# A decoder block's branch projections moved from the attention into the gate pairs, with the first stage reordered and the pooling spread

## The chip, the cores and the metric

The kernel runs on one core of one Trainium2 chip. The metric is the device time of one execution in microseconds (us). Engines are named as in the profile: PE (TensorE, matmuls) with PEld (its weight loads), DVE (VectorE), ACT (ScalarE), POOL (GpSimd), SP (SyncE, which issues most DMAs).

## The reference

One layer on x of 1024 positions by 1024 channels, float32:

```python
h = rmsnorm(x, attn_norm_g)
z = h @ w_in                       # u, v | xb | q | k | values
gates = sigmoid(h @ w_gate + b_gate)
y_a = gmlp_mixer(z[..., :512])     # gelu, layer norm, causal 128x128 mixing
y_b = pool_mixer(z[..., 512:768])  # causal means over 2, 4, 8, 16 positions, 64x64 maps
y_c = diff_attn_mixer(...)         # 4 heads, difference of two softmaxes
merged = g_a * (y_a @ proj_a) + g_b * (y_b @ proj_b) + g_c * (y_c @ proj_c)
x = x + merged @ w_out
x = x + conv_ffn(rmsnorm(x, ffn_norm_g), ...)
return rmsnorm(x, final_norm_g)
```

`proj_a` and `proj_b` are 256 x 1024, `w_gate` is 1024 x 3072 (1024 columns for each of the branches a, b and c).

## The kernel before

Activations lie transposed: a tile has 128 channels by 1024 positions. Each fp32 operand is split into a high and a low part (`split`: an ACT cast and a DVE subtraction), and a product is three matmuls of 512 columns (`mm3`, L189, which records at L191: high x high, high x low, low x high).

`strassen_pair` (L253) multiplies two 128-column blocks of a weight with h by a Winograd form: seven products of twelve matmuls, A11·B11, S1·T1, S2·T2, A12·B21, S3·T3, A22·T4 and S4·B22, which come to stand in the banks b1 to b4. ACT copies b1 after some of them (`c`), DVE adds the copy and another bank (`add`, L262) into the results F1 and F2. S4·B22 goes on top of bank b3, so it waits until b3 has been read into F2, which needs the copy taken after S3·T3. Between products the function calls `mid()`, through which other work can be put in. `prepare` (L226) loads a pair's weights (r1, r2), forms the sums s1, s2 on POOL (L234 to L237) and splits everything; these tiles come from a pool of 13 (`w4`), results from a pool of 34 (`a4`).

The stages, in order of time:
- First stage, up to 118 us: projections for u and v of branch a in two halves of positions, with `scaled` (L314, cast `hb` and its rest), `squares` (L326, ACT) and `factors` (L337: the sums of squares and 1/rms R8, by ACT's square root for the first half and by DVE alone for the second), `bcast_rows` (RB, the factor of each position), `u_gelu`, `v_gelu`, the relative bias `rel_bias` (L380), then the attention's values by Winograd products (T tiles from `h.winograd`).
- The pair with branch b's input `zb`, then three pairs for q and k. `pooling` (L602) is a generator of DVE steps over `zb`: at each `mid` of the first of these pairs two steps are taken. `store_qk` (L671) multiplies by RB (`times_r`, L349), splits and stores to DRAM. `pool_outs` does branch b's small products and stores y_d[2..3]; `gating` has stored branch a's y_d[0..1].
- Twelve gate pairs, about 205 to 435: `strassen_pair`, `times_r` on POOL (L351), a sigmoid on ACT (L771), a store to g_d. g_d 0 to 7 are the gates of branch a, 8 to 15 of b, 16 to 23 of c.
- The last pair of q and k, and the attention, 447 to 602: 35 steps over 32 tiles. In each step `next(filler)` (L1222) does one unit of `merge_ab` (L1164): six matmuls of a branch's projection (`mm`), and DVE's product with the loaded gate tile (L1174). After both branches of a tile an accumulating DMA adds gb to ga.
- Branch c's merge, `w_out`, and the feed-forward part, which the change does not touch.

The order of each engine's instructions is set by the tile framework, which schedules the program with a timeline of its own; `tc.issue_after(x)` holds a group behind the instruction x, `tc.high_priority()` puts one ahead.

## Time and profile before

| | |
|---|---|
| time, median of 3 runs | 1393.08 us (1388.32 to 1394.64) |
| profiled execution | 1393.11 us, its span 1391.4 us |
| granted clock of PE, mean | 0.989 |
| busy: PE, DVE, ACT, POOL | 1346.7, 966.5, 653.0, 496.3 us |
| DMA | 204.63 MB, mean 147 GB/s |

The profile is one execution. Busy times are shares of the span. A timeline row gives start, duration, engine, line, operation, tiles and shapes, and in brackets how long the engine sat idle before it and what released it; rows of a line's group give the count, the busy time, the mean of one in ns, and the idle time ahead. PEclk is the granted clock, 1.00 for 2.4 GHz.

### The profile page before, as it was taken

What the parts mean: (1) busy time and instruction counts of PE and PEld (TensorE: products, weight loads), DVE (VectorE), ACT (ScalarE), POOL (GpSimd) and SP (SyncE); (2) the same over time, 40 slices, a digit from 0 to 9 for tenths busy, and PEclk for the clock granted to TensorE, in tenths of its full rate; (3) what the DMA queues carried; (4) which work ended last, traced back from release to release, by engine and by line L of the source; (5) the groups of instructions that cost most, each with busy time, mean ns of one, the idle gap of its engine ahead of it and who ended that gap; (6) DMA issues with size and microseconds to landing.
All of it is one profiled execution on the core that took longest, in us unless ns stands there. A gap on an engine that the chain in (4) does not pass through costs nothing.

```text
span 1391.4 us, 17681 instructions
## 1 busy us (share of the span) xinstructions
PE 1346.7 (97%) x6454; PEld 1124.1 (81%) x6454; DVE 966.5 (69%) x1481; ACT 653.0 (47%) x1110; POOL 496.3 (36%) x327
## 2 busy tenths in 40 slices
PE   8999899999999889999999999999999999999997
PEld 7888678888888678878878888888888887878786
DVE  7585755544444789967869667667767669985863
ACT  8443244433344567742676443333334336455461
POOL 0005334555553100012231566666666640102014
PEclk9999999999999999999999999999999999999998
DMA  7222244333337898498795222222222248945853
GB/s 262 68 58 108 101 147 151 116 106 111 116 122 184 271 266 232 130 272 189 204 235 122 91 76 88 70 85 91 76 92 79 75 144 303 292 123 150 225 128 124
DMA packets 78830, 204.63 MB, mean 147 GB/s; under 512 B 8270, under 2 KB 17614, under 8 KB 78744
## 3 DMA queue, kind: packets, MB, share of 16 engines
q1 hardware_dynamic: 67224, 180.44, 39.2%
q0 software_dynamic: 11520, 23.07, 9.5%
q8 instruction: 50, 0.82, 0.2%
q14 instruction: 36, 0.29, 0.1%
HBM read 143.70 MB, written 47.46 MB: 137 GB/s over the span
## 4 chain that ended last, share of the span: by engine, by line
PE 68%; DVE 14%; DMA 8%; issue 6%; ACT 3%; POOL 1%; SPq 0%; DVEq 0%; POOLq 0%; ACTq 0%
PE b L191 63%; DMA x<-in_xT 2%; PE mm L191 1%; DMA fr<-in_w_down 1%; DVE sc L757 1%; DVE ft L97 1%; DVE fw L97 1%; DMA qs<-qk_d 1%; DMA fr<-in_w_out 1%; DMA pr<-in_w_proj 1%; PE ms L1107 1%; POOL ga L104 1%; DMA yr<-y_d 1%; ACT fw L96 1%; DMA act<-act_d 1%
## 5 line engine op out<-in xcount | busy, mean ns | idle before, releaser
L191 PE MATMUL b<-ft,fw 128*128 128x512 f32 (+1 forms) x1308 | 293.4, 384 | 6.1 <-ACT ft L96 1.9
L191 PEld LDWEIGHTS b<-ft,fw 128*128 128x128 f32 x1308 | 240.0, 189 | 56.9 <-DVE fw L97 3.2
L351 POOL TENSOR_TENSOR F<-F,RB 128x1024 f32<-128x1024 f32 x68 | 188.5, 2774 | 142.5 <-DVE F L262 141.1
L191 PE MATMUL b<-hb,Ah 128*128 128x512 f32 x608 | 188.8, 390 | 0.0
L262 DVE TENSOR_TENSOR F<-b,c 128x512 f32<-128x512 f32 x152 | 100.8, 682 | 122.4 <-ACT c L281 68.9
L191 PE MATMUL b<-T,Sh 128*128 128x512 f32 x504 | 155.7, 389 | 0.4 <-ACT c L272 0.4
L191 PEld LDWEIGHTS b<-hb,Ah 128*128 128x128 f32 x608 | 114.3, 188 | 23.7
L97 DVE TENSOR_TENSOR Al<-r,Ah 128x1024 fp32r<-128x1024 f32 x38 | 52.2, 1373 | 101.1 <-issue 77.4
L234 POOL TENSOR_TENSOR s<-r 128x512 f32<-128x512 f32 x36 | 54.4, 1512 | 189.1 <-DMA r<-in_w_up 88.9
L191 PE MATMUL b<-hb,Al 128*128 128x512 f32 x304 | 118.3, 389 | 0.0
L97 DVE TENSOR_TENSOR Sl<-s,Sh 128x1024 fp32r<-128x1024 f32 x76 | 109.2, 1437 | 11.7 <-PE b L191 6.1
L96 ACT CAST Sh<-s 128x1024 fp32r<-128x1024 f32 x76 | 80.1, 1053 | 79.4 <-PE b L191 47.5
L191 PEld LDWEIGHTS b<-T,Sh 128*128 128x128 f32 x504 | 94.5, 188 | 20.5 <-ACT c L272 0.8
L191 PE MATMUL b<-hb,Sh 128*128 128x512 f32 x304 | 95.8, 397 | 8.1 <-DVE F L262 8.1
L191 PE MATMUL b<-T,Sl 128*128 128x512 f32 x252 | 98.1, 389 | 0.0
L96 ACT CAST Ah<-r 128x1024 fp32r<-128x1024 f32 x38 | 39.9, 1050 | 109.3 <-PE b L191 104.2
L96 ACT CAST fw<-fr 128x512 fp32r<-128x512 f32 x90 | 54.7, 622 | 60.1 <-DVE fw L97 23.9
L191 PE MATMUL b<-Tl,Sh 128*128 128x512 f32 x204 | 79.4, 389 | 0.0
L191 PE MATMUL b<-Th,Sh 128*128 128x512 f32 x204 | 78.8, 391 | 0.0
L191 PE MATMUL b<-Th,Sl 128*128 128x512 f32 x204 | 78.2, 389 | 0.0
L191 PEld LDWEIGHTS b<-hb,Sh 128*128 128x128 f32 x304 | 57.9, 191 | 21.3 <-DVE F L262 9.4
L97 DVE TENSOR_TENSOR A<-r,A 128x512 fp32r<-128x512 f32 x38 | 72.3, 1904 | 0.0
(284 smaller groups left out, 2829.6 us busy)
## 6 DMA issues: line engine op xcount, KB each, us to landing
fr<-in_w_down SPq DMA_DIRECT2D x47, 512.0 KB, 4.6
r<-in_w_up SPq DMA_DIRECT2D x42, 512.0 KB, 3.6
r<-in_w_gate SPq DMA_DIRECT2D x24, 512.0 KB, 3.8
g_d<-F SPq DMA_DIRECT2D x24, 512.0 KB, 2.6
act_d<-cv SPq DMA_DIRECT2D x22, 512.0 KB, 2.6
act<-act_d SPq DMA_DIRECT2D x22, 512.0 KB, 7.4
fr<-in_w_out SPq DMA_DIRECT2D x18, 512.0 KB, 4.6
ssb<-sq POOLq DMA_DIRECT2D x24, 256.0 KB, 4.1
```

The source lines that it names most:

```text
L96: nc.scalar.copy(hi, src)
L97: (eng or nc.vector).tensor_tensor(out=lo, in0=src, in1=hi.bitcast(F32), op=ALU.subtract)
L104: nc.gpsimd.dma_start(out=dst, in_=src, accum_op=ALU.add)
L191: last_mm[0] = nc.tensor.matmul(ps, lhsT=w[a], rhs=x[b], start=first and i == 0, stop=last and i == 2, skip_group_check=more)
L234: eng.tensor_tensor(out=s1[:, :NH], in0=a21, in1=a22, op=ALU.add)
L262: nc.vector.tensor_tensor(out=o, in0=ps, in1=c, op=ALU.add)
L351: (eng or nc.gpsimd).tensor_tensor(out=F, in0=F, in1=RB, op=ALU.mult)
L757: nc.vector.tensor_tensor_reduce(out=sc_[:, c0:c0 + n], in0=ps[:, :n], in1=H["T"][:, o:o + n], scale=1.0, scalar=mx[:, 0:1] if n_ else 3.0e38,
L1107: nc.tensor.matmul(po[:, :P], lhsT=AH[t][:, kb, :], rhs=H["V"][:, kb, :], start=kb == 0, stop=kb == i)
```

## The change

- First stage: the squares follow the last high cast of their half (`last_hi`); 1/rms of the first half no longer uses ACT's square root; `rel_bias` moves behind the pair of `zb`; the differences in `h.winograd` follow the first half's factors (`r8_done`).
- Pooling: one step at each `mid`, over the first two q/k pairs; `pool_outs` follows in the third.
- Gate pairs 0 to 3 (branch a's gates): the branch's two values (`load_y`) and, for each pair, a weight block (`load_branch`) are loaded; behind a pair, `branch` multiplies 4 x 6 matmuls, two banks of PSUM (`m`) taking turns, and DVE multiplies the gates by them. It is handed on as the `mid` of the next pair, and what is left is done at that pair's end. `times_r` of these pairs is on DVE, F2 ahead of F1, and g_d gets the products instead of the gates.
- Attention: the filler has branch b only, 16 units in place of 32; the accumulating DMA adds g_d[m] from DRAM to gb; two values and four weight blocks are loaded instead of four and eight.

```diff
--- before.py
+++ after.py
@@ -311,11 +311,13 @@
         if j == 1 and kt == 0:
             tc.keep_in_program_order(i)
 
+    last_hi, r8_done = [None], [None, None]
+
     def scaled(kt, j):
 
         src = xt[kt][:, half(j)]
         t = a4([P, 2, NH], F32R, "hb")
-        nc.scalar.mul(t[:, 0, :], src, col(C_GA + kt))
+        last_hi[0] = nc.scalar.mul(t[:, 0, :], src, col(C_GA + kt))
         nc.vector.scalar_tensor_tensor(out=t[:, 1, :], in0=src, scalar=col(C_GA + kt), in1=t[:, 0, :].bitcast(F32),
                                        op0=ALU.mult, op1=ALU.subtract)
         h.b[kt][j] = t[:, 0, :], t[:, 1, :]
@@ -328,7 +330,8 @@
         k = 2 * j + kt % 2
         src = xt[kt][:, half(j)]
         sq = c2("acc" if kt < 2 else "sq")
-        nc.scalar.activation(out=sq, in_=src, func=AF.Square)
+        with tc.issue_after(last_hi[0].ins):
+            nc.scalar.activation(out=sq, in_=src, func=AF.Square)
         if kt < 2:
             acc[k] = sq
         else:
@@ -341,7 +344,7 @@
             ss_cols(ps, acc[2 * j], 4, 1, 0)
             t = tiny(4, "ssum")
             nc.vector.tensor_scalar(out=t, in0=ps[:, :4], scalar1=1.0 / D, scalar2=1e-6, op0=ALU.mult, op1=ALU.add)
-            nc.vector.tensor_copy(R8[:, 4 * j:4 * j + 4], rsqrt(t, 4, j == 0))
+            r8_done[j] = nc.vector.tensor_copy(R8[:, 4 * j:4 * j + 4], rsqrt(t, 4, False))
 
     def gain(kt):
         nc.scalar.mul(xt[kt], xt[kt], col(C_GA + kt))
@@ -466,7 +469,6 @@
         else:
             w_V = load_V()
             wk, wsm, pbd = load_wide()
-            rel_bias()
             factors(1)
             pv = [v_part(1, 0)]
         with tc.high_priority():
@@ -651,8 +653,10 @@
             nc.scalar.mul(yb, pb, col(C_PS + f))
             nc.sync.dma_start(out=y_d[2 + f, :, half(j)], in_=yb)
 
-    for j in range(4):
-        h.winograd(xt, j)
+
+    with tc.issue_after(r8_done[0].ins):
+        for j in range(4):
+            h.winograd(xt, j)
     vs = values()
     next(vs)
     layer_norm()
@@ -667,6 +671,8 @@
     for z in zb:
         times_r(z, nc.vector)
 
+    rel_bias()
+
 
     def store_qk(i, Fs, eng=None):
         for n_, F in enumerate(Fs):
@@ -689,11 +695,10 @@
         ops = prepare(w_qk[1 + i])
         if i == 0:
             pl = pooling(zb)
-        store_qk(i, strassen_pair(ops, h, pb1, lambda: (next(pl, None), next(pl, None))), nc.vector)
-        if i == 0:
+        store_qk(i, strassen_pair(ops, h, pb1, lambda: next(pl, None)), nc.vector)
+        if i == 1:
             for _ in pl:
                 pass
-        if i == 1:
             pl = pool_outs()
 
     for _ in pl:
@@ -763,13 +768,55 @@
         nc.scalar.activation(out=sc_[:, :W], in_=sc_[:, :W], func=AF.Exp, bias=nm_, scale=-1.0, accum_out=sum_)
         st[t]["s"].append(sum_)
 
+    def load_y(i):
+
+        alloc = a4 if i % 2 == 0 else w4
+        hi, lo = alloc([P, 2, NH], F32R, "yv"), alloc([P, 2, NH], F32R, "yv")
+        for j in range(2):
+            raw = c2("yr")
+            nc.sync.dma_start(out=raw, in_=y_d[i, :, half(j)])
+            split(hi[:, j, :], lo[:, j, :], raw)
+        return [(hi[:, j, :], lo[:, j, :]) for j in range(2)]
+
+    def load_branch(n):
+
+        m, g = 2 * n % 8, 2 * (n // 4)
+        raw = c2("pr")
+        nc.sync.dma_start(out=raw.rearrange("p (m a b) -> p m a b", m=2, a=2),
+                          in_=w_proj[m:m + 2, :, g:g + 2, :].rearrange("m p a b -> p m a b"))
+        hl = w4([P, 2, NH], F32R, "ph")
+        split(hl[:, 0, :], hl[:, 1, :], raw)
+        return hl[:, 0, :], hl[:, 1, :]
+
+    def branch(n, Fs, whl, yb):
+
+        for k in (1, 0):
+            F = Fs[k]
+            for j in range(2):
+                ps = pm1()
+                for ki in range(2):
+                    mm3(ps, wsl(whl, 2 * k + ki), yb[ki][j], ki == 0, ki == 1)
+                nc.vector.tensor_tensor(out=F[:, half(j)], in0=ps, in1=F[:, half(j)], op=ALU.mult)
+                if j == 1:
+                    nc.sync.dma_start(out=g_d[2 * n + k], in_=F)
+                yield
+
+    br = iter(())
     for n_ in range(12):
-        Fs = strassen_pair(w_gate[n_], h, pb1)
-        for k, F in enumerate(Fs):
+        if n_ == 0:
+            yb = [load_y(i) for i in range(2)]
+        if n_ < 4:
+            whl = load_branch(n_)
+        Fs = strassen_pair(w_gate[n_], h, pb1, lambda: next(br, None))
+        for _ in br:
+            pass
+        for k, F in reversed(list(enumerate(Fs))):
             m = 2 * n_ + k
-            times_r(F)
+            times_r(F, nc.vector if n_ < 4 else None)
             nc.scalar.activation(out=F, in_=F, func=AF.Sigmoid, bias=col(C_BG + m), scale=1.0)
-            nc.sync.dma_start(out=g_d[m], in_=F)
+            if n_ >= 4:
+                nc.sync.dma_start(out=g_d[m], in_=F)
+        br = branch(n_, Fs, whl, yb) if n_ < 4 else iter(())
 
 
     zero = tiny(1, "zero", 1)
@@ -1156,26 +1203,24 @@
 
     def ab(m):
         if m not in abs_:
-            abs_[m] = a4(n="ga"), a4(n="gb"), load_p(m, 0)
-            nc.sync.dma_start(out=abs_[m][0], in_=g_d[m])
-            nc.sync.dma_start(out=abs_[m][1], in_=g_d[8 + m])
+            abs_[m] = a4(n="gb"), load_branch(4 + m // 2) if m % 2 == 0 else abs_[m - 1][1]
+            nc.sync.dma_start(out=abs_[m][0], in_=g_d[8 + m])
         return abs_[m]
 
     def merge_ab():
         for m in range(KT):
-            ga, gb, whl = ab(m)
+            gb, whl = ab(m)
             for j in range(2):
                 if j == 1 and m < KT - 1:
                     ab(m + 1)
-                for g, k in ((ga, 0), (gb, 2)):
-                    ps = pmm()
-                    for ki in range(2):
-                        mm3(ps, wsl(whl, k + ki), yab[k + ki][j], ki == 0, ki == 1)
-                    nc.vector.tensor_tensor(out=g[:, half(j)], in0=ps, in1=g[:, half(j)], op=ALU.mult)
-                    if (g, j) == (gb, 1):
-                        accumulate(ga, gb)
-                        mg.append(ga)
-                    yield
+                ps = pmm()
+                for ki in range(2):
+                    mm3(ps, wsl(whl, 2 * (m % 2) + ki), yab[ki][j], ki == 0, ki == 1)
+                nc.vector.tensor_tensor(out=gb[:, half(j)], in0=ps, in1=gb[:, half(j)], op=ALU.mult)
+                if j == 1:
+                    accumulate(gb, g_d[m])
+                    mg.append(gb)
+                yield
 
     filler = merge_ab()
     avs = iter(())
@@ -1207,7 +1252,7 @@
     for t in range(len(tiles) + 3):
         hd, i = tiles[min(t, 31)]
         if t == 0:
-            yab = [load_yab(i) for i in range(4)]
+            yab = [load_yab(2 + i) for i in range(2)]
         if t == 2:
             store_qk(NHEAD - 1, last_qk)
         if t % 8 == 3 and t < 24:
@@ -1218,7 +1263,7 @@
             scores(t, 0)
         transpose(t - 2, 0)
         next(avs, None)
-        if t >= 1:
+        if t in (1, 2, 3) or t % 2 == 0:
             next(filler, None)
         scores(t, 1)
         combine(t - 1)
```

Three places show how instructions move.

**DVE in the first q/k pair.** `pw` are the tiles of the pooling steps; F_210 (before) and F_208 (after) are the pair's F2, whose first sum S4·B22 waits for. Before:

```order
L615 TENSOR_TENSOR pw_1511<-pw_1492 128x1022
L620 TENSOR_TENSOR h_207_1487<-h_207_1487,F_183_1338 128x16
L614 COPY pw_1514<-pw_1511 128x4
L615 TENSOR_TENSOR pw_1514<-pw_1511 128x1020
L621 SCALAR_TENSOR_TENSOR F_183_1338<-pw_1468,cs,F_183_1338 128x1024
L614 COPY pw_1531<-pw_1514 64x8
L615 TENSOR_TENSOR pw_1531<-pw_1514 64x1016
L623 COPY F_183_1338<-h_207_1487 128x16
L262 TENSOR_TENSOR F_210_1509<-b_1438,c_1507 128x512
L262 TENSOR_TENSOR F_210_1509<-b_1517,c_1507 128x512
```

After:

```order
L262 TENSOR_TENSOR F_204_1473<-b_1474,c_1441 128x512
L625 COPY F_174_1318<-h_209_1508 128x16
L97 TENSOR_TENSOR Al_1568<-r_216_1557,Ah_1567 128x1024
L97 TENSOR_TENSOR Sl_1572<-s_218_1561,Sh_1571 128x1024
L97 TENSOR_TENSOR A_224_1575<-r_217_1558,A_224_1575 128x512
L97 TENSOR_TENSOR Sl_1579<-s_219_1562,Sh_1578 128x1024
L616 COPY pw_1624<-pw_1527 128x2
L617 TENSOR_TENSOR pw_1624<-pw_1527 128x1022
L262 TENSOR_TENSOR F_208_1506<-b_1443,c_1504 128x512
L262 TENSOR_TENSOR F_208_1506<-b_1513,c_1504 128x512
L616 COPY pw_1642<-pw_1624 128x4
L617 TENSOR_TENSOR pw_1642<-pw_1624 128x1020
```

Ten pooling instructions stood between the pair's first sum and F2's; now the next pair's four splits and three pooling instructions do.

**SP between the q/k pairs and the gate pairs.** `qh` and `ql` are the split results of a q/k pair, `yb` branch b's values, `yr` the reads of branch a's values, `pr` a projection's weights. Before:

```order
L229 DMA r_244_1706<-in_w_qk 128x1024
L230 DMA r_245_1707<-in_w_qk 128x1024
L679 DMA qk_d<-qh_1554 128x1024
L680 DMA qk_d<-ql_1555 128x1024
L679 DMA qk_d<-qh_1561 128x1024
L680 DMA qk_d<-ql_1562 128x1024
L229 DMA r_276_1865<-in_w_gate 128x1024
L230 DMA r_277_1866<-in_w_gate 128x1024
L229 DMA r_296_1996<-in_w_gate 128x1024
```

After:

```order
L777 DMA yr_1876<-y_d 128x512
L777 DMA yr_1882<-y_d 128x512
L777 DMA yr_1886<-y_d 128x512
L785 DMA pr_1890<-in_w_proj 128x2x256
L685 DMA qk_d<-qh_1857 128x1024
L229 DMA r_286_1895<-in_w_gate 128x1024
L230 DMA r_287_1896<-in_w_gate 128x1024
L686 DMA qk_d<-ql_1858 128x1024
L685 DMA qk_d<-qh_1864 128x1024
```

The first gate weights stood behind the stores of the first q/k pair (`qh_1554` to `ql_1562`); now behind the first store of the third one (`qh_1857`).

**PE at the end of a gate pair.** In before this is gate pair 1's end: b_2036 is its bank b3, with S4·B22 on hb and Sh; b_2225 and b_2152 belong to the pair behind it. Before:

```order
L191 MATMUL b_2225<-Th_700,A_324_2145 128x512
L191 MATMUL b_2225<-Tl_701,A_324_2145 128x512
L191 MATMUL b_2225<-Th_700,A_324_2145 128x512
L191 MATMUL b_2225<-Th_712,A_324_2145 128x512
L191 MATMUL b_2152<-Th_700,Sh_2141 128x512
L191 MATMUL b_2152<-Tl_701,Sh_2141 128x512
L191 MATMUL b_2036<-hb_346,Sh_2017 128x512 x2
L191 MATMUL b_2036<-hb_346,Sl_2018 128x512
L191 MATMUL b_2036<-hb_349,Sh_2017 128x512 x2
```

After, gate pair 1's end: b_2054<-Th,Sh is the end of S3·T3, b_2069 the bank b3, m_2312 the third unit of the branch:

```order
L191 MATMUL b_2054<-Th_711,Sh_2050 128x512
L191 MATMUL b_2054<-Tl_712,Sh_2050 128x512
L191 MATMUL b_2054<-Th_711,Sl_2051 128x512
L191 MATMUL b_2069<-hb_351,Sh_2050 128x512 x2
L191 MATMUL b_2069<-hb_351,Sl_2051 128x512
L191 MATMUL b_2069<-hb_354,Sh_2050 128x512 x2
L191 MATMUL b_2069<-hb_354,Sl_2051 128x512
L191 MATMUL b_2069<-hb_357,Sh_2050 128x512 x2
L191 MATMUL b_2069<-hb_357,Sl_2051 128x512
L191 MATMUL b_2069<-hb_360,Sh_2050 128x512 x2
L191 MATMUL b_2069<-hb_360,Sl_2051 128x512
L191 MATMUL m_2312<-yv_1870,ph_2026 128x512
```

S4·B22 stood among the products of the pair behind it; now it follows its own pair's S3·T3, and the branch's matmuls follow it.

## Rows read from the trace of the kernel before

**Rows 1.** Engine line of the page: busy us (share of the span) xinstructions.

```profile
PE 1346.7 (97%) x6454; PEld 1124.1 (81%) x6454; DVE 966.5 (69%) x1481; ACT 653.0 (47%) x1110; POOL 496.3 (36%) x327
```

**Rows 2.** By stretch: us; busy PE, PEld, DVE, ACT, POOL; PEclk, DMA share, GB/s.

```profile
175.00:210.00 35.00, 35.00 (x148) 27.56 (x148) 20.20 (x20) 13.97 (x19) 12.24 (x10) 1.00 0.43 156
455.00:490.00 35.00, 29.57 (x160) 24.34 (x159) 24.75 (x63) 19.93 (x47) 5.81 (x3) 0.95 0.85 267
490.00:525.00 35.00, 30.59 (x195) 25.82 (x194) 30.90 (x101) 22.91 (x67) 1.73 (x2) 1.00 1.03 258
525.00:560.00 35.00, 34.66 (x220) 30.00 (x219) 32.38 (x104) 24.49 (x76) 1.72 (x2) 1.00 0.88 232
560.00:595.00 35.00, 35.00 (x231) 31.42 (x230) 33.28 (x108) 25.74 (x77) 1.72 (x2) 1.00 0.45 135
447.00:602.00 155.00, 142.34 (x862) 121.54 (x861) 129.34 (x408) 101.97 (x291) 12.29 (x11) 0.99 0.81 223
```

**Rows 3.** Timeline of PE: start, us, instruction, in brackets the idle time ahead and releaser.

```profile
13.65 1.28 PE L191 MATMUL b<-hb,wh 128*128 128x512 f32 x3 [1.81 <-ACT hb L318]
49.76 0.58 PE L191 MATMUL b<-wh,hb 128*128 128x256 f32 x1 [1.88 <-ACT vg L429]
159.43 1.22 PE L191 MATMUL b<-hb,Sh 128*128 128x512 f32 x2 [5.49 <-DVE F L262]
453.96 0.73 PE L191 MATMUL b<-hb,Sh 128*128 128x512 f32 x2 [1.40 <-DVE F L262]
```

**Rows 4.** Busy time by stretch again, around and behind the stalls of PE.

```profile
70.00:105.00 35.00, 32.69 (x245) 31.48 (x245) 30.19 (x50) 16.59 (x25) 1.43 (x2) 0.95 0.21 62
13.65:19.00 5.35, 5.30 (x15) 3.90 (x16) 5.35 (x10) 5.35 (x9) 0.00 (x0) 0.68 1.01 367
49.80:52.70 2.90, 2.90 (x14) 2.90 (x14) 1.60 (x8) 2.12 (x5) 0.00 (x0) 0.50 0.03 9
159.50:165.00 5.50, 5.50 (x13) 4.39 (x14) 4.42 (x8) 1.91 (x3) 0.62 (x1) 0.50 0.00 0
454.00:456.00 2.00, 2.00 (x9) 1.66 (x10) 1.78 (x5) 0.00 (x0) 0.80 (x1) 1.00 1.05 389
```

**Rows 5.** Timeline of DVE, first qk pair: a pooling step, and the sum behind them all.

```profile
146.06 1.21 DVE L615 TENSOR_TENSOR pw<-F 128x1023 f32<-128x1023 f32 x1
158.70 1.27 DVE L262 TENSOR_TENSOR F<-b,c 128x512 f32<-128x512 f32 x2
```

**Rows 6.** Timeline of PE, thirteen matmuls of 512 columns without a gap.

```profile
1157.11 3.11 PE L191 MATMUL b<-ft,fw 128*128 128x512 f32 x13
```

**Rows 7.** SyncE's issue of the first gate weights; the page's group of such loads.

```profile
178.94 0.33 SPq L229 DMA_DIRECT2D r<-in_w_gate  x1
...
r<-in_w_gate SPq DMA_DIRECT2D x24, 512.0 KB, 3.8
```

**Rows 8.** Durations: DVE groups 144 to 215, ScalarE groups 175 to 435, one DVE instruction.

```profile
L262 DVE TENSOR_TENSOR F<-b,c 128x512 f32<-128x512 f32 x13 | 8.7, 685 | 19.7 <-PE b L191 10.9 <-ACT c L281 8.7
...
187.17 1.23 DVE L351 TENSOR_TENSOR F<-F,RB 128x1024 f32<-128x1024 f32 x1
...
L96 ACT CAST Ah<-r 128x1024 fp32r<-128x1024 f32 x13 | 13.6, 1045 | 26.7 <-PE b L191 26.7
L771 ACT ACTIVATE F<-F,cs 128x1024 f32<-128x1024 f32 x22 | 25.4, 1155 | 37.9 <-POOL F L351 37.9
```

**Rows 9.** Timeline of GpSimd: two sums of weight blocks.

```profile
154.24 2.24 POOL L236 TENSOR_TENSOR s<-r,r 128x512 f32<-128x512 f32 x1
183.84 1.29 POOL L234 TENSOR_TENSOR s<-r 128x512 f32<-128x512 f32 x1 [6.05 <-DMA r<-in_w_gate]
```

**Rows 10.** DVE groups in the attention, 447 to 602.

```profile
L1174 DVE TENSOR_TENSOR ga<-mm,ga 128x512 f32<-128x512 f32 x16 | 11.0, 686 | 4.8 <-DMA ga<-g_d 2.7 <-PE mm L191 1.9
L97 DVE TENSOR_TENSOR ph<-pr,ph 128x512 fp32r<-128x512 f32 x11 | 7.5, 686 | 0.3 <-ACT ph L96 0.3
L97 DVE TENSOR_TENSOR yv<-yr,yv 128x1024 fp32r<-128x1024 f32 x2 | 2.8, 1382 | 3.4 <-ACT yv L96 3.4
```

## The prediction

> **What bounds the kernel now.** I read the page first: TensorE (PE) is busy 1346.7 of 1391.4 us, 97% [rows 1]. The change removes no multiplication, it only moves some, so all that it can win or lose is in the 44.7 us in which PE idles and in the stretches in which it runs at its lower clock. The table by stretch comes next, since it says where those are: while the gate pairs run PE is full, 35.00 of 35 us at clock 1.00 (the stretch shown is the first of seven like it), with VectorE (DVE) at 20 us and ScalarE at 14 [rows 2]. The attention, 447 to 602, has holes: PE 29.57 and 30.59 of 35 us in its first two stretches, with the DMA queues at 0.85 and 1.03, then 34.66 and 35.00, with DVE at 32.38 and 33.28 [rows 2]. PE's timeline then gives the large single stalls and who ended them: 1.81 us at 13.65 (ScalarE's `hb`), 1.88 at 49.76 (ScalarE's `vg`), 5.49 at 159.43 and 1.40 at 453.96 (both DVE's sum `F`, L262) [rows 3]. The clock by stretch says what they cost on top: 0.68, 0.50 and 0.50 behind the first three (0.50 is the lower level, 1.2 GHz), 1.00 behind the fourth [rows 4]. One matmul of 512 columns costs 0.227 us, (3.11 - 0.39) / 12 [rows 6].
>
> **Part A, first stage.** The squares now follow the last `hb` cast, so at 13.65 no square that waits for x stands ahead of a cast that PE wants. In reach are 1.81 us and 5.35 x 0.32 = 1.7 of clock; the casts still wait for x to land, so I take 2.0. At 49.76 the first four factors' square root leaves ScalarE and the broadcast of RB moves up on PE, with 24 matmuls behind it; in reach are 1.88 + 2.9 x 0.50 = 3.3, and I take 3.0. From 70 to 105 PE idles 2.31 us and loses 35 x 0.05 = 1.75 by its clock [rows 4]; the relative bias leaves this stretch and the second half's factors come earlier, which removes part of DVE's queue there; half is 2.0. The bias' three matmuls are only moved, into the first qk pair, where PE is full: no gain, no loss. Sum **-7.0**; bounds -3 (no clock comes back) and -10.9 (all of it).
>
> **Part B, pooling.** At 159.43 PE waits for the sum of bank `b` that S4·B22 writes over. That sum (L262, 158.70) stands on DVE behind the steps of pooling, the first long one of them 1.21 us at 146.06 [rows 5]. In the change only one step is taken at a `mid` call, and half of them go to the next pair. On PE, A11 of the following pair and more (28 matmuls, 6.4 us) now stand ahead of S4·B22. In reach are 5.49 + 5.5 x 0.50 = 8.2 us [rows 3, 4]. What is late next is ScalarE: the copy of a bank now stands behind the three casts of the relative bias; for this I leave 1.5. Sum **-6.7**; bounds -8.2 and -3.
>
> **Part C, from the last early qk pair to the first gate pair.** Before, the first gate weights are issued at 178.94, a whole pair ahead [rows 7]. After, SyncE issues them behind `qk_d<-qh_1857`, a store that waits for the end of the pair: its last sum 0.69, the multiplication by RB 1.23, ScalarE's `qh`, taken as long as its cast `Ah`, 1.05 [rows 8]. Then two issues of 0.33, the landing 3.8 [rows 7] and the cast `Ah` 1.05 [rows 8]: 8.5 us in which PE has only 12 branch matmuls, 2.7 us. The sums that S1 needs (two of 1.29 on GpSimd, [rows 9]) and their cast run while A11's 12 matmuls do. So PE idles 5.8 us; the nearest stall, 5.49, was followed by 5.5 us at clock 0.50, a loss of 2.7 [rows 3, 4]. Sum **+8.5**; bounds +5 (no clock lost, the store a little earlier) and +13 (the values read back from DRAM come late too).
> In this hole GpSimd's sums run beside DVE's multiplications and splits, and the rows show two prices for such a sum: 1.29 us at 183.84, with DVE idle, and 2.24 at 154.24, beside DVE's pooling steps [rows 9]. The Trainium skill, SBUF — State Buffer, "Who interferes with whom", says that a DVE instruction with two SBUF inputs contends with a GpSimd instruction that reads SBUF, and the loser waits for the whole of the other; by that rule the two sums are slow here and the total is 1.9 us higher. I keep the lower price in the sum, because DVE waits for PE, and so is mostly idle, while the weights land; the other price is a rival below.
>
> **Part D, ends of gate pairs 0, 1 and 2.** Before, S4·B22 of a pair stands inside the next pair's matmuls. After, it follows S3·T3 directly and must wait for the sum that needs S3·T3. The same order stands in the trace once, at 453.96: 1.40 us [rows 3]. The branch matmuls behind it have two PSUM buffers, both filled earlier, and wait for the first gate product: from the end of that wait, DVE sums 0.69, times RB 1.23, ScalarE's sigmoid 1.16, DVE's product 0.69 [rows 8, 10], 3.77 in all, less S4·B22's 12 x 0.227 = 2.72: 1.05 us. So 2.45 at each of three ends: **+7.4**. Bounds +4 (part of it covered) and +15 (the clock drops by half for some 5 us each time).
>
> **Part E, the moved work.** 96 matmuls, 96 x 0.227 = 21.8 us, are added to a stage in which PE was full: all of it lengthens that stage. DVE's added work there (eight multiplications by RB, taken from GpSimd, 16 products, splits) costs nothing while it has 15 of 35 us free [rows 2]; were that cover gone it would be 8 x 1.23 + 16 x 0.69 = 21 us. The attention loses the 21.8 us on PE, and on DVE 16 products (11.0 us), two value splits of 1.38 and four weight splits of 0.69: 16.5 us [rows 10]. What comes off its 155 us? If DVE set the pace at its present share, 129.34 / 155 = 0.834, the gain would be 16.5 / 0.834 = 19.8. If every hole went and PE ran at the rate of its last 70 us (0.995), the stage would take (142.34 - 21.8) / 0.995 = 121 us, 34 less. If PE kept its share, 0.918, it would be 23.7. I take 25, near the last, since eight loads of 512 KB and two of the branch values leave a DMA queue that was full, and PE idles 9.8 us in those 70 us [rows 2]. Sum 21.8 - 25 = **-3.2**; bounds +2 and -12.
>
> **Sum.** -7.0 - 6.7 + 8.5 + 7.4 - 3.2 = -1.0 us. The profiled execution took 1393.11 us, 1.7 more than its span and 0.03 above the median, so I forecast **1392 us**: no change that a measurement of this kernel tells from none (0.5%, 7 us, so 1386 to 1400).
>
> **The rivals.**
> *The attention opens up (faster).* All its holes go, and it runs at the rate of its last 70 us. For it: PE and DVE are both above 92% there, and the two poor stretches are those with the DMA queues at 0.85 and above [rows 2]. Against it: the loads of the next heads stay, and DVE's chain per tile does too. 34 instead of 25: **1383 us**.
> *The holes between pairs are small (faster).* If the store ahead of the gate weights were ready earlier, and half of C and D were covered: 1392 - 8 = **1384 us**. Against it: the chains are made of durations from rows and the order is fixed.
> *Each gate pair's weights come late (slower).* The branch keeps one value tile and up to two weight tiles in the pool of 13 weight buffers. If the next pair's loads can only start when S4·B22 has released buffers, each of the three ends pays issue, landing and cast, 0.66 + 3.8 + 1.05 = 5.5, less the 12 branch matmuls' 2.7, and 2.1 of clock (between the 1.45 and the 2.75 that rows 4 give): 4.9 x 3 = 15, **1407 us**. It decides as soon as the loads of gate pair 1 start after the end of pair 0. For it: a pair uses eleven such tiles. Against it: SyncE has these loads directly behind the last qk stores.
> *GpSimd's sums at the slow price in the hole.* 2 x 0.95 = 1.9 more: **1394 us**. By the skill's rule this is the case to expect whenever DVE is busy; the trace agrees at 154.24.
> That the change does not do what it says I leave out: the moves stand in the order of the instructions.
>
> **Chances.** My sum 0.33 (its own range 1384 to 1400; faster 0.09, same 0.22, slower 0.02); attention opens 0.27 (faster 0.22, same 0.05); weights late 0.23 (slower 0.20, same 0.03); small holes 0.09 (0.07 faster, 0.02 same); slow sums 0.08 (0.07 same, 0.01 slower). Together faster 0.38, same 0.39, slower 0.23. The range, 1376 to 1408, goes from the faster rivals with A and B at their better bounds to the slow rival; it leaves some 2 in 10 outside.
>
> **What would show it.** Right: the stalls of 1.8, 1.9 and 5.5 us are gone from PE's timeline before 165; a PE stall of 5 to 7 us ahead of the first `b<-hb,Ah` of the gate pairs, with the clock at half behind it; stalls of about 1.4 and 1 us at three pair ends; the gate stage about 38 us longer (21.8 + 8.5 + 7.4); and an attention some 25 us shorter. Wrong: an attention shorter by 30 or more, or by less than 20; a pair end with a stall above 4 us released by a DMA; stalls of the first stage that only move.

## The result, and the profile after

| | before | after |
|---|---|---|
| time, median | 1391.19 us (4 runs) | 1431.72 us (4 runs, 1427.39 to 1433.51) |
| ratio | | 1.0269, interval 1.0242 to 1.0296 |
| span of the profiled execution | 1391.4 us | 1425.5 us |

The change makes the kernel 2.7% slower, outside the forecast range of 1376 to 1408. All ratios here are of fast runs, which leaves out one run of 5419.56 us of the kernel with the first stage alone. The page of after first, engine line; it answers to [rows 1]:

```profile
PE 1354.4 (95%) x6454; PEld 1123.6 (79%) x6454; DVE 961.4 (67%) x1497; ACT 651.8 (46%) x1111; POOL 473.4 (33%) x319
```

PE has as many matmuls as before and 71.1 us of idle time in place of 44.7. Its timeline (rows with the idle time ahead and its releaser) says where; it answers to [rows 3]:

```profile
12.99 0.51 PE L191 MATMUL b<-hb,wh 128*128 128x512 f32 x1 [1.30 <-ACT hb L320]
...
147.93 0.80 PE L191 MATMUL b<-hb,Al 128*128 128x512 f32 x1 [2.47 <-DVE Al L97]
...
204.05 5.73 PE L191 MATMUL m<-yv,ph 128*128 128x512 f32 x12 [7.04 <-ACT yv L96]
215.33 0.50 PE L191 MATMUL b<-Th,Sh 128*128 128x512 f32 x1 [2.14 <-ACT Sh L96]
232.22 0.73 PE L191 MATMUL b<-hb,Sh 128*128 128x512 f32 x2 [1.40 <-DVE F L262]
236.63 0.73 PE L191 MATMUL m<-yv,ph 128*128 128x512 f32 x2 [1.38 <-DVE F L799]
...
497.76 0.50 PE L191 MATMUL mm<-yv,ph 128*128 128x512 f32 x1 [2.27 <-ACT ph L96]
...
530.57 0.80 PE L191 MATMUL mm<-yv,ph 128*128 128x512 f32 x1 [3.86 <-DVE gb L1219]
...
683.51 0.77 PE L191 MATMUL b<-ft,fw 128*128 128x512 f32 x1 [6.94 <-DVE gc L1244]
```

The stall at 49.76 is gone and the 5.49 us at 159.43 became 2.47. New are 7.04 ahead of gate pair 0 and 2.14 inside it, 1.40 and 1.38 at its end (two more ends like it follow), 2.27 and 3.86 in the attention, and 6.94 ahead of w_out, where PE did not wait before. Stretches of after (us; busy PE, PEld, DVE, ACT, POOL; clock, DMA share, GB/s): two behind the hole, the attention, two parts of it, and from the attention to w_out:

```profile
204.00:216.00 12.00, 9.30 (x27) 6.43 (x28) 3.95 (x6) 3.34 (x6) 5.81 (x4) 0.78 0.63 230
216.00:232.00 16.00, 14.82 (x59) 11.76 (x57) 3.57 (x5) 2.93 (x6) 5.07 (x4) 0.89 0.25 67
...
492.47:631.09 138.62, 120.96 (x747) 101.50 (x747) 114.46 (x386) 93.47 (x280) 11.85 (x10) 0.98 0.78 202
528.00:560.00 32.00, 26.28 (x156) 21.58 (x157) 25.15 (x84) 18.93 (x56) 1.72 (x2) 0.95 1.06 270
595.00:631.09 36.09, 31.25 (x213) 26.56 (x211) 33.06 (x126) 28.24 (x93) 0.86 (x1) 1.00 0.45 124
631.09:683.51 52.42, 45.48 (x207) 37.46 (x207) 34.14 (x64) 13.37 (x29) 12.98 (x15) 0.97 0.83 219
```

The same two stretches of before, cut at the same instructions (S4·B22 of the last q/k pair, the first matmul of branch c's merge, the first of w_out):

```profile
453.96:601.78 147.82, 136.56 (x836) 117.04 (x836) 128.07 (x405) 97.84 (x284) 10.99 (x9) 0.99 0.80 223
601.78:649.12 47.34, 47.27 (x213) 38.59 (x214) 28.64 (x56) 12.21 (x28) 12.12 (x14) 1.00 0.90 241
```

So the last q/k pair ends 38.5 us later (453.96, 492.47), the attention gives back 9.2 (147.82 less 138.62), and the way to w_out costs 5.1 more. These add to 34.4, the difference of the two profiled spans (34.1). The medians differ by 40.5, since the profiled execution of after was the fastest of its four (1427.39 us).

One profile is one execution, and places in it move from one to the next. Seven kernels of this case (before and six whose edits touch only the attention) reach S4·B22 of the last q/k pair at 448.90 to 453.96, 451.0 on average; before is the latest of them. Four with everything of after up to there reach it at 489.81 to 492.47, 490.7 on average.

### The profile page after: what moved, and what is told of

It is laid out like the page before. It is cut to its first block, busy times and chain, and to the rows that moved or that the text cites. A ratio compares the mean times of both kernels' runs of the same rounds, so it can differ in the third digit from the quotient of the medians.

```text
span 1425.5 us, 17646 instructions
## 1 busy us (share of the span) xinstructions
PE 1354.4 (95%) x6454; PEld 1123.6 (79%) x6454; DVE 961.4 (67%) x1497; ACT 651.8 (46%) x1111; POOL 473.4 (33%) x319
## 4 chain that ended last, share of the span: by engine, by line
PE 60%; DVE 12%; DMA 11%; issue 8%; POOL 5%; ACT 3%; SPq 1%; DVEq 0%; POOLq 0%; ACTq 0%
PE b L191 54%; DMA r<-in_w_gate 3%; DMA gb<-g_d 2%; PE m L191 1%; POOL F L354 1%; PE mm L191 1%; DMA fr<-in_w_down 1%; DVE Al L97 1%; POOL s L235 1%; DVE F L262 1%; DVE sc L762 1%; POOL s L234 1%; POOL gb L104 1%; POOL s L236 1%; DVE fw L97 1%
## 5 line engine op out<-in xcount | busy, mean ns | idle before, releaser
L354 POOL TENSOR_TENSOR F<-F,RB 128x1024 f32<-128x1024 f32 x60 | 164.1, 2738 | 89.5 <-DVE F L262 87.8
L191 PE MATMUL b<-hb,Ah 128*128 128x512 f32 x608 | 191.9, 393 | 0.0
L234 POOL TENSOR_TENSOR s<-r 128x512 f32<-128x512 f32 x36 | 55.5, 1542 | 315.6 <-DMA r<-in_w_gate 128.1
L97 DVE TENSOR_TENSOR Al<-r,Ah 128x1024 fp32r<-128x1024 f32 x38 | 56.8, 1494 | 110.6 <-issue 82.3
L97 DVE TENSOR_TENSOR Sl<-s,Sh 128x1024 fp32r<-128x1024 f32 x76 | 97.6, 1284 | 25.7 <-ACT Sh L96 21.8
L191 PEld LDWEIGHTS b<-T,Sh 128*128 128x128 f32 x504 | 95.3, 189 | 22.2 <-ACT c L272 2.3
L191 PEld LDWEIGHTS b<-hb,Sh 128*128 128x128 f32 x304 | 56.5, 188 | 22.6 <-DVE F L262 10.4
L191 PEld LDWEIGHTS b<-hb,Al 128*128 128x128 f32 x304 | 57.9, 190 | 15.7 <-DVE Al L97 3.7
```

What stands on the lines that cost most here:

```text
L97: (eng or nc.vector).tensor_tensor(out=lo, in0=src, in1=hi.bitcast(F32), op=ALU.subtract)
L191: last_mm[0] = nc.tensor.matmul(ps, lhsT=w[a], rhs=x[b], start=first and i == 0, stop=last and i == 2, skip_group_check=more)
L234: eng.tensor_tensor(out=s1[:, :NH], in0=a21, in1=a22, op=ALU.add)
L354: (eng or nc.gpsimd).tensor_tensor(out=F, in0=F, in1=RB, op=ALU.mult)
```

## The experiments

Sixteen kernels ran, each beside before, in groups of two or four that share a chip. The ratios are to before.

**The first stage and the pooling, each alone and together.** On before:

```diff
-            rel_bias()
             factors(1)
...
+        with tc.issue_after(last_hi[0].ins):
+            nc.scalar.activation(out=sq, in_=src, func=AF.Square)
...
-        store_qk(i, strassen_pair(ops, h, pb1, lambda: (next(pl, None), next(pl, None))), nc.vector)
+        store_qk(i, strassen_pair(ops, h, pb1, lambda: next(pl, None)), nc.vector)
```

> The kernel before with the first-stage part of the change alone (squares behind the casts, no ACT square root, the T differences behind the factors, the relative bias behind the pair of zb). Theory (stage account): the first pair starts 10 us earlier, as in the changed kernel, 2.5 us of which are the moved bias matmuls; the rest stays, so 1391 - 7 = 1384 us. Rival (the gain only moves): the bias' casts on ACT and the late copies make the first q/k pairs wait, and the total stays within 2 us of 1391.

> The kernel before with the spread pooling alone. Together with the first-stage part it measured 0.996, the first-stage part alone 0.999. Theory: the spread pooling takes away the 5.5 us stall and its half clock at 159, as far as A11's wait does not replace them: 1391 - 5 = 1386, so that the first-stage part is worth little with it or without it. Rival: the two need each other, since each alone only moves the wait on DVE: 1391 within 2.

> The kernel before with the first-stage part and the spread pooling, nothing else. The first stage alone gave its 8 us back in the q/k pairs (it measured 0.999 of before). Theory: the spread pooling takes away the part of these waits that stands behind the pooling steps on DVE, so that together they keep 6 to 8 us: 1392 - 7 = 1385. Rival: A11 of the second pair waits for a split behind the pooling steps instead, and both parts together are worth 2 us or less.

The first stage alone took 1392.23 us (0.9991, 0.9978 to 1.0005), the pooling alone 1389.68 (0.9990, 0.9975 to 1.0004), both 1385.41 (**0.9963**, 0.9949 to 0.9978): faster than either of the two kernels of this case. Each alone was expected to gain (7 and 5 us), and the rivals held, within 2 us of before; both together were expected to keep 6 to 8 us and kept 5.8. PE's timeline of the first stage alone:

```profile
145.10 0.50 PE L191 MATMUL b<-Th,Sh 128*128 128x512 f32 x1 [0.70 <-ACT c L272]
149.52 0.73 PE L191 MATMUL b<-hb,Sh 128*128 128x512 f32 x2 [1.40 <-DVE F L262]
156.25 1.22 PE L191 MATMUL b<-hb,Ah 128*128 128x512 f32 x2 [3.72 <-ACT Ah L96]
163.17 0.50 PE L191 MATMUL b<-Th,Sh 128*128 128x512 f32 x1 [1.06 <-ACT Sh L96]
```

The pair of zb starts there at 107.80 in place of 118.39, but the bias' matmuls follow, and these four stalls, 6.9 us, with one of 0.82 at 141.38, stand where 5.49 stood. With both parts 2.48 is left, besides 0.82 and 0.59. The pooling alone has 3.08 at 156.38, on DVE's `Al`, and 0.55. The last q/k pair comes at 449.50 with the first stage alone, at 450.29 with the pooling alone and at 445.19 with both; without either it came at 448.90 to 453.96. So only both together are earlier than all of these: each alone moves the wait.

**The gate pairs.** First the operands of a pair ahead of the branch's loads, then the branch's matmuls held in program order, each on after:

```diff
+        ops = prepare(w_gate[n_])
         if n_ == 0:
             yb = [load_y(i) for i in range(2)]
...
-                ps = pm1()
+                with tc.issue_after(last_mm[0].ins):
+                    ps = pm1()
...
```

> The changed kernel, with each gate pair's operands prepared ahead of the branch's loads in program order, so that they take the earlier buffers. Theory: the 7.0 us hole ahead of gate pair 0, the 2.1 us behind it with their half clock, and the three pair ends of 2.8 us each all come from weights that are loaded late; 13.7 + 8.5 = 22 us go, to about 1410. Rival: only the order of loads at the first pair is cured and the pair ends stay, 1432 - 12 = 1420. Second rival: the wait moves to the branch's own loads, 1430.

> The changed kernel, with each unit of branch a's matmuls held behind the matmul ahead of it in program order, so that the scheduler can't put them early; loads as in the changed kernel. Theory: the pair ends (three of 2.8 us) come from early units that hold both PSUM banks, and go, while the hole ahead of gate pair 0 stays, longer by the 12 matmuls that ran in it: 1432 - 8.5 + 2.7 = 1426. Rival: the pair ends come from the weights of the next pair: no change, 1432 or more.

With the operands ahead: 1408.91 us (1.0110, 1.0083 to 1.0137), 22.8 less than after by the medians, as expected (the two did not share a chip; S4·B22 of the last q/k pair comes at 470.32 and 492.47, 22.2 apart). PE's only stall above 0.7 us from 197 to the last q/k pair is

```profile
215.66 1.20 PE L191 MATMUL m<-yv,ph 128*128 128x512 f32 x4 [1.90 <-DVE yv L97]
```

With the matmuls held: 1442.66 us (1.0361, 1.0342 to 1.0379), 11 more than after. The first expectation fell, the rival held. Its timeline of PE:

```profile
209.84 1.22 PE L191 MATMUL b<-hb,Ah 128*128 128x512 f32 x2 [11.72 <-ACT Ah L96]
...
235.10 0.73 PE L191 MATMUL b<-hb,Ah 128*128 128x512 f32 x2 [0.96 <-ACT Ah L96]
237.32 0.50 PE L191 MATMUL b<-hb,Al 128*128 128x512 f32 x1 [1.49 <-DVE Al L97]
...
268.23 0.50 PE L191 MATMUL b<-hb,Al 128*128 128x512 f32 x1 [3.85 <-DVE Al L97]
```

The early branch matmuls of the changed kernel were not the cause of the pair ends; they filled time in which the next pair's weights were not there. The cause is the order: where the branch's tiles come ahead, each pair's weights are late. SyncE's issues of gate pair 1's first weights, in after and with the operands ahead:

```profile
217.29 0.33 SPq L229 DMA_DIRECT2D r<-in_w_gate  x1
```
```profile
203.62 0.42 SPq L229 DMA_DIRECT2D r<-in_w_gate  x1
```

In after SyncE waited 11.8 us there for DVE's split `A` of pair 0 (L97), which reads pair 0's own weights: a buffer of the pool of 13 had to come free. For gate pair 0 its queue held it up, behind the store `qk_d<-qh`: 200.53, against 174.80 with the operands ahead. The edit moves the buffers and the place in the queue together, and no run changed the number of buffers, so the share of each is not shown.

**The first unit of the filler.** On after, and with it loads a unit earlier:

```diff
-        if t in (1, 2, 3) or t % 2 == 0:
+        if t in (1, 2, 3) or t and t % 2 == 0:
...
-                if j == 1 and m < KT - 1:
+                if j == 0 and m < KT - 1:
                     ab(m + 1)
```

> The changed kernel, with the filler's first unit in step 1 instead of step 0 of the attention. Theory: in step 0 that unit is the first to take banks of the attention's PSUM pool, so the banks of `mm` come to lie where w_out's first banks are opened later, and these wait for the last products of the merge; with the first unit in step 1 the 6.9 us stall ahead of w_out goes, and the 2.3 us stall ahead of the first unit as well: 1432 - 7 = 1425, at most 1423. Rival: the tail's stall comes from DVE's queue, whatever banks are used: within 2 us of 1432.

> As the run with the first unit in step 1, and the next gate tile and weights are loaded one unit earlier. Theory: the 3.9 us stall of PE (5.6 on DVE) behind a late gate tile goes: 4 us faster than the run with the first unit in step 1. Rival: the DMA queue is full there, and an earlier load makes the heads' loads late instead: the same time within 2 us.

> The changed kernel with all three repairs: operands prepared ahead of the branch's loads, the first unit in step 1, loads a unit earlier. Theory: the costs add: 1409 - 7 - 4 = 1398, still no faster than before, since PE's 21.7 us in the gate pairs come back only in part. Rival: with its holes gone the attention gives back the whole 21.7 us and the first stage's gain shows: 1385.

The first unit in step 1: 1416.77 us (1.0189, 1.0160 to 1.0218), 15 less than after by the medians; the profiled spans, 1425.5 and 1415.8, differ by 9.7, and the two kernels did not share a chip, so the size is known to some 5 us. The two stretches, the second one ending at w_out:

```profile
490.36:626.12 135.76, 118.77 (x747) 102.72 (x747) 114.13 (x385) 93.18 (x280) 11.92 (x10) 0.96 0.81 207
626.12:671.42 45.30, 45.30 (x206) 37.60 (x207) 27.53 (x54) 11.21 (x25) 11.27 (x13) 1.00 0.82 228
```

PE waits for nothing ahead of w_out, and that way is 7.1 us shorter than in after. One unit in step 0 cost that much 180 us later. What PE waits for in after is a product of branch c's merge, read from a bank `mm`; the second line is the DMA that adds the product to its tile:

```profile
682.68 0.69 DVE L1244 TENSOR_TENSOR gc<-mm,gc 128x512 f32<-128x512 f32 x1
```
```profile
683.66 0.86 POOL L104 DMA_DIRECT2D gb<-gc  x1 [2.15 <-DVE gc L1244]
```

PE went on at 683.51, before that DMA was issued, so it did not wait for the sum: what fits is that w_out's first bank was that `mm`, as the theory says (a profile does not name banks). All five kernels with a unit in step 0 (after, operands ahead, matmuls held, and the two with the changed filler on before) have 6.8 to 8.5 us there, and the twelve with their first unit later have none. Loads a unit earlier: 1414.63 us (1.0175, 1.0157 to 1.0193), no clear gain; its rival held. All three repairs: 1395.98 us (1.0032, 1.0016 to 1.0047), as expected (1398): the costs add, and what is left is still not faster than before.

The same earlier loads on the kernel with first stage and pooling (the edit of `j` above, nothing else) brought nothing either, 1385.60 (0.9964, 0.9948 to 0.9981).

> The kernel before with the first-stage part, the spread pooling, and gate tiles and weights loaded one unit earlier in the attention. Theory: PE's stalls of 1 to 2 us per late gate tile between 455 and 505 go: 1385 - 3 = 1382. Rival: the DMA queue is full there, and nothing changes: 1385.

**What the attention gives back.** On before, the changed filler alone; the same without the accumulation; no filler work at all; then DVE's or PE's part of branch a alone, and the gate tiles' loads:

```diff
-                for g, k in ((ga, 0), (gb, 2)):
+                ps = pmm()
...
-                    accumulate(gb, g_d[m])
...
+                    if g is gb:
+                        nc.vector.tensor_tensor(out=g[:, half(j)], in0=ps, in1=g[:, half(j)], op=ALU.mult)
...
-            nc.sync.dma_start(out=abs_[m][0], in_=g_d[m])
+            nc.gpsimd.memset(abs_[m][0], 0.5)
```

> The kernel before with the changed filler alone (branch b only, 16 units, the accumulation from g_d); branch a's projection and product are left out everywhere. It prices the attention's relief by itself. Theory: DVE and the DMA queue pace the attention, and it gives back only what it did in the changed kernel, 9 to 10 us, to about 1382. Rival: the removed 21.7 us of PE work come back nearly whole, and the changed kernel lost them by what it did to the order ahead of the attention: 1391 - 22 = 1369.

> As the kernel with the changed filler alone, and without the accumulation of g_d from DRAM as well (left out). Theory: the accumulation is hidden; within 3 us of the run with it. Rival: reading 512 KB per tile from DRAM through the accumulating queue is what holds the attention: 8 us or more faster than with it.

> The kernel before with no filler matmuls, products or accumulations at all in the attention (branches a and b are left out, the gate tiles of b are still loaded), so it shows what the attention takes by itself. In the changed kernel taking out 21.7 us of PE work shortened it by 9 to 13. Theory: DVE's own work and the heads' loads set its length, and PE's share is not what counts: the 43.4 us of PE work are worth no more than 28, so 1364 or more. Rival: PE counts and the loss lay in holes that late gate tiles opened, so nearly all of it comes back, 1391 - 40 = 1351.

The changed filler alone: 1386.23 us (0.9961, 0.9939 to 0.9982), 6 us for 21.8 of PE work; without the accumulation 1383.08 (0.9926, 0.9901 to 0.9951), 3 less, at the edge of what was expected. Without any filler work: 1371.37 us (0.9862, 0.9838 to 0.9886), 20 us for 43.4. The attention of the changed filler alone with its way to w_out, and the attention without filler:

```profile
450.30:587.87 137.57, 120.37 (x746) 101.79 (x746) 114.32 (x386) 93.65 (x280) 11.90 (x10) 0.98 0.80 202
587.87:640.16 52.29, 45.49 (x206) 37.45 (x207) 34.11 (x64) 13.60 (x29) 13.02 (x15) 0.96 0.83 220
```
```profile
449.68:569.72 120.04, 101.81 (x651) 84.35 (x651) 102.43 (x366) 90.24 (x276) 4.79 (x2) 0.96 0.69 180
```

The first attention is 10.3 us shorter than before's, about as expected (9 to 10), but its first unit is in step 0 too, and the way to w_out gives 5.0 of it back (52.29, 47.34). Without filler some 8 us are lost again behind the start of w_out (750.5 us from there to the end, 742.3 in before), which is why the whole gains 20.

For the attention itself all 32 units together are worth 147.8 - 120.0 = 27.8 us, 0.87 each, where a unit takes PE 1.36. Half of them, at that price, 13.9; measured 10.7 to 12.9 in the changed kernels with the first unit in step 1. My theory for this was that the length follows DVE's work (25.6 us less of it in the last run, 13.8 in the first). Two runs took one engine's work away at a time:

> The kernel before without DVE's 16 products of branch a in the attention (left out); PE's matmuls, all loads and the accumulations stay. It takes 11.0 us from DVE and nothing from PE. Theory (the attention's length follows DVE's work): 147.8 us become 137 to 139, the time 1391 - 10 = 1381. Rival (it follows PE's work): no change within 2 us.

> The kernel before without PE's 96 matmuls of branch a in the attention (left out); DVE's 16 products stay, with the gate tile in place of the bank, and all loads and accumulations stay. It takes 21.7 us from PE and nothing from DVE. Theory (the length follows DVE's work): 3 us or less, so 1389 or more. Rival (it follows PE's work as far as DVE lets it): 10 us or more, 1381 or less.

The theory fell. Without DVE's 11 us: 1389.85 (0.9987, 0.9966 to 1.0007), the attention 145.5. Without PE's 21.7: 1402.65 (1.0070, 1.0045 to 1.0095), slower. Its attention, and a stall in it:

```profile
450.66:605.37 154.71, 126.13 (x740) 104.48 (x741) 126.09 (x401) 96.34 (x281) 11.36 (x9) 0.92 0.81 215
```
```profile
489.03 1.29 DVE L1176 TENSOR_TENSOR ga<-ga 128x512 f32<-128x512 f32 x2 [6.71 <-DMA ga<-g_d]
```

DVE's product, which no matmul held back any longer, stood in its queue ahead of the next tile's scores and waited for a gate tile; PE waited 5.90 us behind it. More of PE's waits were for the filler's own weights `ph`, 10.6 us in four stalls where before had 2.7 in two:

```profile
PE mm L191 <- ACT ph L96: 10.6, 4, 4.0
```

Between these stalls PE ran at a clock of 0.92 instead of 0.99. Its busy time fell from 136.56 to 126.13 us, by 10.4 where 21.8 of work had gone, so the clock cost it some 11 us. So this run does not say what PE's work alone is worth: it also made loads late. The last two runs took the gate tiles' loads away:

> The kernel before with the 16 gate tiles of branches a and b not loaded in the attention (POOL sets them to a constant instead; the gates are left out of the products); every matmul, product and accumulation stays. It takes 8 MB of the some 33 MB off the queues. Theory (late loads make the holes, and the lower clock behind them): the stalls between 455 and 505 go, 8 us or more: 1383 or less. Rival (the order of the heads' own work makes them): within 3 us of 1391.

> The changed kernel with the first unit in step 1, without the loads of branch b's gate tiles and without the accumulation from DRAM (both left out, as are the gates of b), matmuls and products as they are. Theory (late loads): its attention, 135.8 us with them, falls by 10 or more, to 126 or less, and PE's clock there rises from 0.96 to near 1.00: 1417 - 10 = 1407 or less. Rival: it stays above 132 us, since the heads' own loads and products set the pace: 1413 or more.

From before: 1386.30 us (0.9953, 0.9937 to 0.9969), the attention 141.8, 6 less, no stall above 0.3 us left between 460 and 591: late loads are part of it. From the changed kernel with the first unit in step 1: 1418.33 (1.0186, 1.0162 to 1.0211) with an attention of 140.2: nothing won, though the DMA share between 526 and 561 fell from 1.06 to 0.62 (525 to 560 in the run with the loads). In the first run the gain fell between theory and rival; in the second the rival held. But the second run is no proof that late loads cost nothing, since other loads were late in it, blocks of the filler's weights:

```profile
528.36 1.22 PE L191 MATMUL mm<-yv,ph 128*128 128x512 f32 x2 [4.49 <-ACT ph L96]
```
```profile
527.69 0.62 ACT L96 CAST ph<-pr 128x512 fp32r<-128x512 f32 x1 [5.60 <-DMA pr<-in_w_proj]
```

From 526 to 545 PE's clock was 0.82 there.

## Why the prediction was wrong

| term | predicted | measured | by |
|---|---|---|---|
| A + B, first stage and pooling | -13.7 | -5.8 | both parts alone |
| C + D, gate pairs' weights and ends | +15.9 | +22.8 | operands ahead; 23.2 by the stalls and clock of after |
| E, branch work moved | -3.2 | +9 to +11 | 21.8 less an attention 10.7 to 12.9 shorter, with the first unit in step 1 |
| first unit in step 0 | not seen | +10 to +15 | first unit in step 1 |
| sum | -1.0 | +36 to +43 | +40.5 by the medians |

The step that failed most is E, "What comes off its 155 us? ... I take 25": 10.7 to 12.9 came off, and 9.2 in after. A unit that takes PE 1.36 us cannot bring more than that unless holes close as well, and I had 25 for 16 of them, 1.56 each. That holes would rather open than close could have been asked of [rows 2]: PE idled in two of four stretches of before with all its filler, so part of that filler ran in time in which PE would have waited anyway. The runs show 0.87 per unit, and no run that took away DVE's work, PE's or the gate loads by itself shortened the stage by more than 6.1 us. The bound "If DVE set the pace", 19.8, was itself too kind: the measured relief, 9.2, lies under both ends of that term.

C was right in its mechanism and 6 us short. From the end of the last q/k products (197.03) to the first stall at gate pair 0's end (230.82) PE took 33.8 us for 84 matmuls, which take 19.1 at 0.227 each: 14.7 us were lost and not 8.5. PE idled 7.04, 0.39 and 2.14 us of it and not 5.8; the clock, 0.78 for 12 us and 0.89 for 16 more, cost the other 5.1 and not 2.7. The hole was longer since the gate weights issued at 200.53 let `Ah` start at 208.29, 7.4 us behind that issue's end, not the 3.8 of [rows 7]. The branch's values, weights and the stores were on the way with them (DMA share 0.87 from 198.0 to 208.3); no run took these away alone. The 2.14 come from GpSimd: S1 waits for L234 and L235, and C had both done while A11 ran, but L236 stood between them. The slow price came true for one of the sums, beside DVE's `Al`:

```profile
209.37 1.23 DVE L97 TENSOR_TENSOR Al<-r,Ah 128x1024 fp32r<-128x1024 f32 x1 [3.33 <-ACT Ah L96]
```
```profile
209.65 2.08 POOL L234 TENSOR_TENSOR s<-r 128x512 f32<-128x512 f32 x1 [37.96 <-DMA r<-in_w_gate]
211.69 1.29 POOL L236 TENSOR_TENSOR s<-r,r 128x512 f32<-128x512 f32 x1
212.94 1.26 POOL L235 TENSOR_TENSOR s<-s,r 128x512 f32<-128x512 f32 x1
```

That is 0.8 of the 1.9 us. The Trainium skill, SBUF — State Buffer, "Who interferes with whom", says that a DVE instruction with two SBUF inputs contends with a GpSimd instruction that reads SBUF, and the trace agrees with it here: the first sum overlapped `Al` by 0.95 us and took 0.79 longer, and the next, behind `Al`, took 1.29.

D was right to some 0.4 us per end in its size (2.78, 2.84 and 2.84 us, not 2.45) and in the waits themselves: 1.40 for DVE's sum and 1.38 for its first gate product, with the clock at 1.00. What it took as given was the order PE has there. That order is what the scheduler made of late weights: the run with the matmuls held shows the waits behind it, and with the operands ahead all three ends are gone. So the rival "weights come late" had the cause of C and D together, at 22.8 us, but neither its price nor its sign came true: gate pair 1's loads start at 217.29, before the end of pair 0 (about 235), and no pair end waits above 4 us.

A was right about what goes and too high in its size. The pair of zb starts 10.0 us earlier in after (118.39, 108.40), of which the moved bias matmuls (six in the trace, not three) are 2.4. But with the first stage of before it starts at 114.56 to 118.39 in eight kernels, 116.2 on average, and with the changed one at 107.67 to 110.30 in ten, 108.9 on average: 7.3, less 2.4, is 4.9 and not 7.0. Part of the 7.0 was clock that only some executions lose. All eight have the stall of 1.88 us at the place of 49.76; behind it the clock was 0.50 or 0.51 in three of them, before among them, and 1.00 in five, such as the changed filler alone:

```profile
49.62:52.50 2.88, 2.88 (x23) 2.77 (x23) 1.60 (x9) 2.12 (x5) 0.00 (x0) 1.00 0.04 9
```

B was wrong about what stays: its "one step is taken at a mid call" left `Al` of the second pair behind pooling steps, 2.47 us and some 1.5 of half clock, and 0.82 behind ACT, 4.8 us in place of 1.5. And the parts need each other: alone neither is worth anything that can be measured.

The step into w_out was in no term, since the order of the instructions there had not changed; the banks had, by the reading above.

## What to carry to other kernels

Price moved filler by what its stage would lose without it, not by the engine time it takes: filler that runs in holes gives back less than it costs elsewhere, here 0.87 of 1.36 us a unit against the full 1.36 in a stage whose PE is full. Where a change puts long-lived tiles into a small pool ahead of a prefetch, count the buffers first: the order of the two loads was worth 23 us here. Look at a stall's clock in more than one execution before it is priced. Two parts that feed one queue are measured together as well as alone.

## What the runs showed that I had not expected

The first unit to take a tile from a PSUM pool changed what the first tiles of the next pool waited for: one unit moved by one step took 7.1 us off a stretch that ends some 180 us later. And taking work from PE can cost time, by the order and the clock that follow: without 96 of its matmuls the attention was 6.9 us longer, with 10.6 us of waits for late weights and at a granted clock of 0.92 instead of 0.99. The same stall of 1.88 us was followed by a clock of 0.50 in some executions and of 1.00 in others; what decides it is open.

What stays open: what sets the 120 us of the attention without filler, and what the changed kernel's attention would take with none of its loads late; each such edit lets the scheduler order the stage anew, and no run held that order fixed.
